# Prompt output rows and last states' keys: PE transposes replaced by VectorE 32x32 blocks and placing transfers to DRAM

## The chip, the cores and the metric

The kernel runs on one core of a Trainium2 chip. Time is device microseconds of that core for one launch; three runs of the kernel before gave a median of 2321.09 us (2320.81 to 2322.24).

## The reference

One decoder layer is computed for two groups of tokens that share the weights: a prompt of 256 tokens and 8 sequences of 8 sample tokens, 320 tokens in all, width 2048. Everything is float32.

```python
proj = jnp.einsum('btd,de->bte', x, w_in)          # q k v i f o | hq hf hi hg | two gates
h, C, n, m = _mlstm(q, k, v, ig, lf, C0, n0, m0)   # 4 heads, keys 256, values 512
h = _unheads((h - mu) * lax.rsqrt(var + LN_EPS)) * ml_norm_g
branch_a = h * jax.nn.sigmoid(ml_o)
o, S = _hgrn2(hq, jnp.log(f), 1.0 - f, hi, S0)     # 8 heads, keys 128, values 256
o = o * lax.rsqrt(jnp.mean(jnp.square(o), axis=-1, keepdims=True) + LN_EPS)
branch_b = _unheads(o) * hg_norm_g * jax.nn.silu(hg_g)
merged = jax.nn.sigmoid(gate_a) * (branch_a @ w_branch_a) + jax.nn.sigmoid(gate_b) * (branch_b @ w_branch_b)
x1 = _layernorm(alpha * x + merged @ w_out)
y = _layernorm(alpha * x1 + jnp.square(jax.nn.relu(x1 @ w_up)) @ w_down)
```

The outputs are `y` for both groups and the new states `C`, `n`, `m`, `S` for both groups. The prompt's last states are `C = (weighted K)^T V` and `S = (weighted K)^T I` over its 256 tokens.

## The kernel before

Activations lie with channels on the partitions and the 320 tokens along the row. A weight tile is 128 output columns; it comes in two units (halves) of 128x1024 values. For each unit SP loads `wr` (three buffers), ACT rounds it to a high part `wh`, DVE subtracts to get the low part `wl` (three pairs of buffers, called `bb` later, when there are more), and PE runs 24 matmuls of 320 columns: high by high, high by low, low by high, for each of 8 slices. A `wr` buffer is reloaded as soon as DVE has read it. This stream of 14,592 matmuls runs from start to end; everything else is fitted into it.

The fitting is done at build time by a small scheduler. Each piece of work (a head's output, a state update, an eviction) is a generator that yields instructions with an engine, an assumed cost and waits; the scheduler holds a model clock for each engine and issues a piece's next instruction between two groups of three matmuls once the model says that its inputs are there. So the order on each engine is fixed in the program, and real waits are semaphores. All transfers but a few go out on SP's queue in that order: weight reloads, state loads and stores, and the spills to DRAM named below.

Four places matter here, with the lines of the profile:

- **mLSTM output.** `m_num` (prompt rows) and `m_sample` (sample rows) of each of the 4 heads leave normalised rows in `hb`: three 128-token groups by 512 values. To turn them into channels by tokens, PE transposes 128x128 blocks into a PSUM bank (L1175, 12 for each head), ACT evicts them, multiplied by the norm weight `ml_norm_g`, and SP stores four tiles `hT` of 128x320.
- **HGRN2 output.** `h_out` of each of the 8 heads does the same from `on` (three groups by 256 values; L1610, 6 for each head), to tiles `oT`, with `hg_norm_g`.
- **Last states' keys.** `m_KW` weights the prompt's keys, PE turns them (L993, 4 for each mLSTM head), ACT and DVE split them into high and low parts `khl`, and `m_CP` stores them to `kD` with the values in `vD`. `h_sp` turns the HGRN2 keys (L1559, 2 for each head), ACT evicts them, and SP stores keys and values to `sD`. At the very end `m_C` (loads on POOL's queue) and `h_S` bring them back for the final state matmuls.
- **The gates.** Later `ev_o` (branch a) and `ev_hg` (branch b) evict the gate projections, take the stored tile that `fetch` has loaded and multiply the two.

Of the kernel before, what the change touches and what calls it, by code (L numbers as in the profile page):

```python
# [284 lines left out]


def by_row(ap, off, gap):

    return cap(ap, off, [[32, 4], [8, 2], [1, 8]] if gap else [[8, 4], [32, 2], [1, 8]])
# [16 lines left out]
class Program:  # L306
# [48 lines left out]
    def carve(self):  # L355
# [43 lines left out]
        self.pb = Pool([A(800)])  # L399
        self.ktk = Pool([A.three(2, 128)])  # L400
        self.it2 = [B.three(3, 256) for _ in range(2)]
# [221 lines left out]
    def start(self):  # L623
# [54 lines left out]
        self.gb_ev = [Ev() for _ in range(KT)]  # L678
        self.hT = [self.dr.tile([128, TOK], F32, name=f"hT{j}") for j in range(KT)]
        self.oT = [self.dr.tile([128, TOK], F32, name=f"oT{j}") for j in range(KT)]  # L680
        self.hT_ev = [Ev() for _ in range(KT)]
# [56 lines left out]
    def lb(self):  # L738

        nc = self.nc  # L740
        v = self.vec[:, V_LB:V_LB + 16].rearrange("p (r h) -> p r h", r=2)
        m = yield acq(self.sm)
        lb = self.lbv.rearrange("p (r h) -> p r h", r=2)
        e = m[:, 0:16].rearrange("p (r h) -> p r h", r=2)
        mx = m[:, 16:24]
        yield ("dve", 80, lambda: nc.vector.tensor_tensor(mx, v[:, 0], v[:, 1], ALU.max))
        yield ("dve", 80, lambda: nc.vector.tensor_tensor(e, v, mx.unsqueeze(1).to_broadcast([128, 2, 8]), ALU.subtract))
        yield ("act", 110, lambda: self.A(e, e, AF.Exp))
        yield ("dve", 80, lambda: nc.vector.tensor_tensor(mx, e[:, 0], e[:, 1], ALU.add))
# [3 lines left out]
        yield rel(self.sm, m)  # L753
        g, b = self.vec[:, V_G1:V_G1 + 16], self.vec[:, V_B1:V_B1 + 16]
# [80 lines left out]
    def m_start(self, h):  # L835
# [5 lines left out]
        m["v"] = [Ev() for _ in range(4)]  # L841
        for n in ("E", "S", "Vt", "Vs", "KW", "KH", "KS", "N", "CP", "QW", "bc_", "vst", "S0", "C", "ld"):
            m[n] = Ev()
# [132 lines left out]
    def m_KW(self, h):  # L976
# [12 lines left out]
        khl = yield acq(self.khl)  # L989
        b = yield acq(self.sbank)  # L990
        for i in range(2):
            for c in range(2):
                yield ("pe", PE_T, lambda: nc.tensor.transpose(b[:, 256 * i + 128 * c:256 * i + 128 * c + 128], kw[:, c, 128 * i:128 * i + 128], self.ident))  # L993
# [4 lines left out]
        yield ("dve", dve(512, True), lambda: v.tensor_tensor(kl, bv, kh.bitcast(F32), ALU.subtract))  # L998
        yield rel(self.sbank, b)
        yield post(m["KH"])  # L1000
# [55 lines left out]
    def m_num(self, h):  # L1056
# [15 lines left out]
        for i in range(2):  # L1072
# [25 lines left out]
    def m_C(self, h):  # L1098
        k = yield acq(self.kx)
        kt = yield ("pool", 1000, lambda: self.nc.gpsimd.dma_start(k, self.kD[h]))  # L1100
        w = yield acq(self.vx)
# [4 lines left out]
        for c in range(2):  # L1106
            if h:
                yield wait(self.ln[1]["fin"])
            b = yield acq(self.mbank)
            yield ("pe", 6 * pe_r(512), lambda: [self.mm(  # L1110
                b, k[:, x, s, 128 * c:128 * c + 128], w[:, y, s, :], start=n == 0, stop=n == 5)
                for n, (s, x, y) in enumerate((s, x, y) for s in range(2) for x, y in ((0, 0), (0, 1), (1, 0)))])
# [15 lines left out]
    def m_sample(self, h):  # L1128
# [41 lines left out]
        yield rel(self.sbank, nb)  # L1170
        yield rel(self.sm, dn)
        for j in range(4):
            b = yield acq(self.sbank)
            for i in range(3):
                yield ("pe", PE_T, lambda: nc.tensor.transpose(b[:, 128 * i:128 * i + 128], hb[:, i, 128 * j:128 * j + 128], self.ident))  # L1175
# [5 lines left out]
            yield rel(self.sbank, b)  # L1181
            yield ("sp", 620, lambda: self.dma(self.hT[jj], o))
            yield post(self.hT_ev[jj])
            yield wait(self.later())
            yield rel(self.tst, o)
        yield rel(self.hb, hb)
# [363 lines left out]
    def h_sp(self, h):  # L1550
# [5 lines left out]
        it, ks = m["it"], m["k"][:, 0:256]  # L1556
        b = yield acq(self.sbank)
        for i in range(2):
            yield ("pe", PE_T, lambda: nc.tensor.transpose(b[:, 128 * i:128 * i + 128], ks[:, 128 * i:128 * i + 128], self.ident))  # L1559
        kt = yield acq(self.ktk)  # L1560
        yield ("act", act(256, True), lambda: self.A(kt, b[:, 0:256].rearrange("p (a k) -> p a k", a=2)))
        yield rel(self.sbank, b)
# [3 lines left out]
        yield rel(self.ktk, kt)  # L1566
        yield post(m["SP"])

    def h_S(self, h):
        x = self.sx[h]  # L1570
        t = yield ("sp", 620, lambda: self.dma(x, self.sD[h]))
        e = Ev()
# [14 lines left out]
    def h_out(self, h):  # L1587
# [11 lines left out]
        for i in range(2):  # L1599
            yield from self.rms(b[:, 256 * i:256 * i + 256], on[:, i, :], 128)  # L1600
        yield rel(self.sbank, b)
        yield wait(m["S"])
        ob = m["ob2"]
        yield from self.rms(ob[:, 0:256], on[:, 2, :], 128)
        yield rel(self.sbank, ob)
        yield rel(self.at, at)
        for j in range(2):
            b = yield acq(self.sbank)
            for i in range(3):
                yield ("pe", PE_T, lambda: nc.tensor.transpose(b[:, 128 * i:128 * i + 128], on[:, i, 128 * j:128 * j + 128], self.ident))  # L1610
            jj = 2 * h + j
            o = yield acq(self.ho)
            g = self.vec[:, V_HGG + jj:V_HGG + jj + 1]
            yield ("act", act(NP_, True, 1), lambda: self.A(o[:, 0:NP_], b[:, 0:NP_], scale=g))
            yield ("act", act(64, True, 1), lambda: self.A(by_row(o, NP_, False), by_row(b, NP_, True), scale=g))
            yield rel(self.sbank, b)
            yield ("sp", 620, lambda: self.dma(self.oT[jj], o))
            yield post(self.oT_ev[jj])
            yield wait(self.later())
            yield rel(self.ho, o)  # L1620
        yield rel(self.on, on)
# [20 lines left out]
    def fetch(self, kind, j):  # L1642
# [4 lines left out]
        x = self.met[kind, j] = yield acq(self.ld)  # L1647
        e.t = yield ("sp", 620, lambda: self.dma(x, src[j]))

# [4 lines left out]
    def ev_o(self, j, c, b):  # L1654
# [32 lines left out]
    def ev_hg(self, j, c, b):  # L1687
# [7 lines left out]
        x = yield from self.fetched("hg", j)  # L1695
        yield ("dve", dve(TOK), lambda: v.tensor_tensor(g, g, x, ALU.mult))
        yield rel(self.ld, x)
# [256 lines left out]
    def run(self, pool):  # L1954
# [8 lines left out]
        self.vx, self.kx, self.main_end = Pool([]), Pool([]), Ev()  # L1963
        self.sD = [self.dr.tile([128, 768], F32, name=f"sD{j}") for j in range(HH)]
        self.kD = [self.dr.tile([128, 2, 2, 256], F32, name=f"kD{j}") for j in range(MH)]
        self.vD = [self.dr.tile([128, 2, 2, 512], F32, name=f"vD{j}") for j in range(MH)]
# [84 lines left out]
```

## Time and profile before

| What | Value |
| --- | --- |
| Median of 3 runs | 2321.09 us (2320.81 to 2322.24) |
| Profiled execution, its time | 2321.41 us |
| Its span | 2319.6 us |
| Granted TensorE clock, mean | 0.999 |
| Busy: PE, DVE, ACT, POOL | 2309.1, 1351.6, 1059.5, 11.9 us |
| DMA | 143275 packets, 424.92 MB, mean 183 GB/s |

All durations below come from the profiled execution, whose span is the time from its first to its last instruction. The stages in it: the mLSTM heads run beside the weight stream from about 75 to 440 us, the HGRN2 heads from about 440 to 860 us, then the gates and branch projections to about 1280 us, then the output projection and the feed-forward part to about 2292 us, and the last states with the final normalisation to the end.

### The profile page before, as it was taken

Reading aid. Unit: us, or ns where it says so; the run is one execution under the profiler, and the core shown is the slowest. Engines: PE = TensorE matmul, PEld = TensorE weight load, DVE = VectorE, ACT = ScalarE, POOL = GpSimd, SP = SyncE. Lnnn points to the kernel's source line nnn. Section 1 sums busy time; section 2 is a strip of 40 time slices with the busy share of each in tenths; the row PEclk is TensorE's granted clock in tenths of the full one; section 3 lists DMA queues with packets and bytes.
Section 4 is the critical chain, followed back from the end, with each engine's and each line's share of the span. In section 5 each row is a group of like instructions: output and inputs, shape, how many; then the busy total and the mean of one; then the engine's idle time right before and its main releaser. Section 6 shows DMA issues by size and latency. Waiting matters only on the chain.

```text
span 2319.6 us, 38982 instructions
## 1 busy us (share of the span) xinstructions
PE 2309.1 (100%) x15808; PEld 2267.0 (98%) x15808; DVE 1351.6 (58%) x2297; ACT 1059.5 (46%) x1703; POOL 11.9 (1%) x37
## 2 busy tenths in 40 slices
PE   9999999999999999999999999999999999999998
PEld 9999999999999999999999999999999999999997
DVE  6566567666666776555555767654444444444455
ACT  5444445555556565444433446533442343234333
POOL 0000000000000000000000000000000000000000
PEclk9999999999999999999999999999999999999999
DMA  7676777555555555555545654444444444444465
GB/s 282 206 254 223 269 280 230 193 187 181 183 181 188 182 189 172 174 177 169 176 169 176 213 167 152 150 146 154 146 155 146 154 147 154 146 153 147 153 219 182
DMA packets 143275, 424.92 MB, mean 183 GB/s; under 512 B 16372, under 2 KB 37748, under 8 KB 142072
## 3 DMA queue, kind: packets, MB, share of 16 engines
q1 hardware_dynamic: 141800, 415.96, 53.9%
q0 software_dynamic: 1152, 6.29, 0.8%
q8 instruction: 123, 2.02, 0.4%
q14 instruction: 56, 0.46, 0.1%
q10 hardware_dynamic: 144, 0.20, 0.0%
HBM read 371.48 MB, written 50.90 MB: 182 GB/s over the span
## 4 chain that ended last, share of the span: by engine, by line
PE 98%; ACT 1%; DVE 0%; DMA 0%; issue 0%; SPq 0%; ACTq 0%; DVEq 0%
PE bank L348 97%; ACT f3m L342 0%; DMA f<-first 0%; PE bank L1610 0%; PE bank L946 0%; PE bank L1175 0%; PE bank L1448 0%; DVE f3m L1938 0%; ACT f L342 0%; PE bank L1453 0%; PE bank L1019 0%; PE bank L1502 0%; PE bank L993 0%; PE bank L1559 0%; ACT oC L342 0%
## 5 line engine op out<-in xcount | busy, mean ns | idle before, releaser
L348 PE MATMUL bank<-xh,wh 128*128 128x320 f32 (+1 forms) x2432 | 782.4, 322 | 0.3 <-ACT wh L342 0.3
L488 DVE TENSOR_TENSOR wl<-wr,wh 128x1024 fp32r<-128x1024 f32 x426 | 522.0, 1225 | 399.6 <-ACT wh L342 395.9
L348 PE MATMUL bank<-xh,wl 128*128 128x320 f32 (+1 forms) x2432 | 752.2, 310 | 0.0
L348 PE MATMUL bank<-xl,wh 128*128 128x320 f32 (+1 forms) x2432 | 749.8, 309 | 0.0
L342 ACT ACTIVATE wh<-wr 128x1024 fp32r<-128x1024 f32 x426 | 451.0, 1059 | 498.1 <-PE bank L348 478.2
L348 PEld LDWEIGHTS bank<-xh,wh 128*128 128x128 f32 x2432 | 457.8, 188 | 19.2 <-issue 14.7
L348 PEld LDWEIGHTS bank<-xl,wh 128*128 128x128 f32 x2432 | 458.1, 189 | 2.9
L348 PEld LDWEIGHTS bank<-xh,wl 128*128 128x128 f32 x2432 | 458.0, 188 | 0.5 <-DVE wl L701 0.3
L488 DVE TENSOR_TENSOR bb<-wr,bb 128x1024 fp32r<-128x1024 f32 x176 | 215.7, 1226 | 229.2 <-ACT bb L342 229.1
L342 ACT ACTIVATE bb<-wr 128x1024 fp32r<-128x1024 f32 x176 | 186.4, 1059 | 313.3 <-PE bank L348 294.9
L348 PE MATMUL bank<-xh,bb 128*128 128x320 f32 (+1 forms) x1280 | 285.4, 309 | 0.0
L348 PE MATMUL bank<-rxb,bb 128*128 128x320 f32 x1208 | 276.3, 309 | 0.0
L348 PE MATMUL bank<-ra,wh 128*128 128x320 f32 x988 | 265.9, 308 | 0.0
L348 PE MATMUL bank<-ra,bb 128*128 128x320 f32 x1096 | 264.2, 308 | 0.7 <-DVE ra L1640 0.7
L348 PEld LDWEIGHTS bank<-xh,bb 128*128 128x128 f32 x1280 | 215.0, 188 | 0.0
L348 PEld LDWEIGHTS bank<-rxb,bb 128*128 128x128 f32 x1208 | 204.3, 188 | 0.2
L348 PE MATMUL bank<-xl,bb 128*128 128x320 f32 (+1 forms) x640 | 197.7, 309 | 0.0
L348 PEld LDWEIGHTS bank<-ra,bb 128*128 128x128 f32 x1096 | 187.1, 188 | 1.2 <-DVE ra L1640 0.9
L348 PEld LDWEIGHTS bank<-ra,wh 128*128 128x128 f32 x988 | 176.3, 188 | 0.0
L348 PE MATMUL bank<-rxb,wh 128*128 128x320 f32 x548 | 169.0, 308 | 0.0
L348 PE MATMUL bank<-rxb,wl 128*128 128x320 f32 x548 | 169.0, 308 | 0.0
L348 PEld LDWEIGHTS bank<-xl,bb 128*128 128x128 f32 x640 | 120.4, 188 | 0.3 <-DVE xl L1863 0.3
(263 smaller groups left out, 2233.9 us busy)
## 6 DMA issues: line engine op xcount, KB each, us to landing
wr<-wt SPq DMA_DIRECT2D x602, 512.0 KB, 3.4
rx<-C SPq DMA_DIRECT2D x34, 256.0 KB, 5.6
Cs<-rx SPq DMA_DIRECT2D x34, 256.0 KB, 4.4
f<-C SPq DMA_DIRECT2D x30, 256.0 KB, 5.3
Cs<-f SPq DMA_DIRECT2D x30, 256.0 KB, 4.8
f<-first SPq DMA_DIRECT2D x6, 704.0 KB, 10.8
vD<-ra SPq DMA_DIRECT2D x4, 1024.0 KB, 6.8
f<-S SPq DMA_DIRECT2D x8, 512.0 KB, 6.6
```

Source lines behind the costliest of these rows:

```text
L342: return self.nc.scalar.activation(out, in_, func, **kw)
L348: self.nc.tensor.matmul(*a, **kw)
L488: self.V().tensor_tensor(lo, raw, hi.bitcast(F32), ALU.subtract)
```

## The change

The prompt's rows no longer go through PE. DVE transposes each 32x32 block inside a tile in place (`v.transpose`); a 128x128 tile is then right inside its 16 blocks but the blocks are in the wrong places. `place` puts them right on the way to DRAM: four transfers, one for each band of 32 partitions, write every 32-value piece of a partition (128 bytes) to its place in a "home" of 128x128 tiles. The sample rows keep their PE transposes and go to small tensors `hL` and `oL`, one transfer for each head in place of the four or two that carried the tiles. A consumer now loads a tile with two transfers, 256 pieces of 512 bytes from `hH` or `oH` and 128 pieces of 256 bytes from `hL` or `oL`. The keys of the last states take the same way: `kD` and `sD` become homes, the HGRN2 values get their own tensor `iD`. The norm weights move from ACT's evictions to the multiplications in `ev_o` and `ev_hg`; `ml_norm_g` is negated once at the start, since `ev_o` had a factor of -1 there.

The diff, without the plain renames and allocations:

```diff
+def cap2(ap, off, dims):
+    return bass.AP(ap.tensor, ap.offset + off, [list(x) for x in dims])
...
+        home = lambda name, heads: [self.dr.tile([2, D // heads, 128], F32, name=f"{name}{j}") for j in range(heads)]
+        tail = lambda name, heads: [self.dr.tile([D // heads, 64], F32, name=f"{name}{j}") for j in range(heads)]
...
+    def place(self, to, x):
+
+        for a in range(4):
+            yield ("sp", 620, lambda: self.dma(to(a), x[32 * a:32 * a + 32]))
+
+    def rows_to(self, home):
+
+        return lambda a: cap2(home, 32 * a, [[128, 32], [32 * 128, home.shape[1] // 16], [1, 32]])
...
         khl = yield acq(self.khl)
-        b = yield acq(self.sbank)
-        for i in range(2):
-            for c in range(2):
-                yield ("pe", PE_T, lambda: nc.tensor.transpose(b[:, 256 * i + 128 * c:256 * i + 128 * c + 128], kw[:, c, 128 * i:128 * i + 128], self.ident))
         m["khl"] = khl
         kh, kl = khl[:, 0], khl[:, 1]
-        bv = b.rearrange("p (a k) -> p a k", a=2)
-        yield ("act", act(512, True), lambda: self.A(kh, bv))
-        yield ("dve", dve(512, True), lambda: v.tensor_tensor(kl, bv, kh.bitcast(F32), ALU.subtract))
-        yield rel(self.sbank, b)
+        yield ("dve", dve(512), lambda: v.transpose(kw[:, :, 0:256], kw[:, :, 0:256]))
+        yield ("act", act(512), lambda: self.A(kh.rearrange("p s k -> p (s k)").rearrange("p (c t) -> p c t", c=2), kw[:, :, 0:256]))
+        yield ("dve", dve(512), lambda: v.tensor_tensor(kl, kw[:, :, 0:256], kh.bitcast(F32), ALU.subtract))
...
             yield rel(self.sbank, b)
+            yield ("dve", dve(512), lambda: v.transpose(hb[:, i, :], hb[:, i, :]))
         yield rel(self.sbank, db)
         yield post(m["N"])
+        yield from self.place(self.rows_to(self.hH[h]), hb[:, 0:2, :].rearrange("p i v -> p (i v)").rearrange("p (b c) -> p b c", c=32))
+        m["hb_"].t = self.s.lands[-1]
...
-        yield ("sp", 620, lambda: self.dma(self.kD[h], m["khl"].bitcast(F32)))
+        x = m["khl"].bitcast(F32).rearrange("p x s k -> p (x s k)").rearrange("p (B k) -> p B k", k=32)
+        yield from self.place(lambda a: cap2(self.kD[h], 32 * a, [[128, 32], [32 * 128, 32], [1, 32]]), x)
...
-        kt = yield ("pool", 1000, lambda: self.nc.gpsimd.dma_start(k, self.kD[h]))
+        kt = yield ("pool", 1000, lambda: self.nc.gpsimd.dma_start(
+            k.rearrange("p x s k -> p (x s k)").rearrange("p (y k) -> p y k", k=128), self.kD[h].rearrange("y p k -> p y k")))
...
+        b = yield acq(self.sbank)
         for j in range(4):
-            b = yield acq(self.sbank)
-            for i in range(3):
-                yield ("pe", PE_T, lambda: nc.tensor.transpose(b[:, 128 * i:128 * i + 128], hb[:, i, 128 * j:128 * j + 128], self.ident))
-            jj = 4 * h + j
-            o = yield acq(self.tst)
-            g = self.vec[:, V_MLG + jj:V_MLG + jj + 1]
-            yield ("act", act(NP_, True, 1), lambda: self.A(o[:, 0:NP_], b[:, 0:NP_], scale=g))
-            yield ("act", act(64, True, 1), lambda: self.A(by_row(o, NP_, False), by_row(b, NP_, True), scale=g))
...
-            yield ("sp", 620, lambda: self.dma(self.hT[jj], o))
+            yield ("pe", PE_T, lambda: nc.tensor.transpose(b[:, 128 * j:128 * j + 128], hb[:, 2, 128 * j:128 * j + 128], self.ident))
+        o = yield acq(self.tst)
+        for j in range(4):
+            yield ("act", act(64, True), lambda: self.A(by_row(o, 64 * j, False), by_row(b, 128 * j, True)))
+        yield rel(self.sbank, b)
+        yield ("sp", 620, lambda: self.dma(
+            self.hL[h].rearrange("(j p) t -> p j t", p=128), o[:, 0:256].rearrange("p (j t) -> p j t", t=64)))
...
-        for i in range(2):
-            yield ("pe", PE_T, lambda: nc.tensor.transpose(b[:, 128 * i:128 * i + 128], ks[:, 128 * i:128 * i + 128], self.ident))
-        kt = yield acq(self.ktk)
-        yield ("act", act(256, True), lambda: self.A(kt, b[:, 0:256].rearrange("p (a k) -> p a k", a=2)))
...
-        yield ("sp", 620, lambda: self.dma(self.sD[h][:, 0:256], kt))
-        yield ("sp", 620, lambda: self.dma(self.sD[h][:, 256:768], it[:, 0:2, :]))
+        yield ("dve", dve(256), lambda: v.transpose(ks, ks))
+        yield from self.place(lambda a: cap2(self.sD[h], 32 * a, [[128, 32], [32 * 128, 8], [1, 32]]),
+                              ks.rearrange("p (b k) -> p b k", k=32))
+        yield ("sp", 620, lambda: self.dma(self.iD[h], it[:, 0:2, :]))
...
+        for i in range(2):
+            yield ("dve", dve(256), lambda: v.transpose(on[:, i, :], on[:, i, :]))
+        yield from self.place(self.rows_to(self.oH[h]), on[:, 0:2, :].rearrange("p i v -> p (i v)").rearrange("p (b c) -> p b c", c=32))
...
+        if isinstance(src[j], tuple):
+            y, z = src[j]
+            yield ("sp", 620, lambda: self.dma(x[:, 0:NP_].rearrange("p (i t) -> p i t", i=2), y.rearrange("i p t -> p i t")))
+            e.t = yield ("sp", 620, lambda: self.dma(x[:, NP_:TOK], z))
...
-        yield ("dve", dve(TOK), lambda: v.scalar_tensor_tensor(g, g, -1.0, x, ALU.mult, ALU.mult))
+        yield ("dve", dve(TOK, ptr=1), lambda: v.scalar_tensor_tensor(g, g, self.vec[:, V_MLG + j:V_MLG + j + 1], x, ALU.mult, ALU.mult))
```

The instruction order shows what this does to the engines. On PE, in the first mLSTM head's output, the order before has this stretch; L1175 are output transposes and L993 key transposes, both removed or thinned, L946 are transposes of the values, which stay, and L348 is the weight stream:

```order
L1175 MATMUL bank_88<-cst,f_77 128x128
L993 MATMUL bank_84<-cst,f_76 128x128
L348 MATMUL bank_83<-xh,wh 128x320
L348 MATMUL bank_83<-xl,wh 128x320
L348 MATMUL bank_83<-xh,wl 128x320
L946 MATMUL bank_87<-cst,f_75 128x128
L1175 MATMUL bank_88<-cst,f_77 128x128
L348 MATMUL bank_83<-xh,wh 128x320
```

In the changed program the same head's output has only the sample rows' transposes (now L1191), and the weight stream (now L352) runs six matmuls between two of them:

```order
L1191 MATMUL bank_88<-cst,f_77 128x128
L352 MATMUL bank_83<-xh,wh 128x320
L352 MATMUL bank_83<-xl,wh 128x320
L352 MATMUL bank_83<-xh,wl 128x320
L352 MATMUL bank_83<-xh,wh 128x320
L352 MATMUL bank_83<-xl,wh 128x320
L352 MATMUL bank_83<-xh,wl 128x320
L1191 MATMUL bank_88<-cst,f_77 128x128
```

Over the whole program PE has 96 transposes fewer and no other instruction more or less.

On SP's queue, at the first mLSTM head's key store, the order before is:

```order
L351 DMA gaD_148<-f_76 128x320
L351 DMA kD_100<-ra 128x1024
L351 DMA vD_104<-ra 128x2048
L351 DMA wr<-wt 128x1024 x2
L351 DMA Cs<-f_77 128x512 x2
```

and in the changed program, at the same place:

```order
L355 DMA gaD_156<-f_76 128x320
L355 DMA kD_108<-ra 32x32x32 x4
L355 DMA vD_112<-ra 128x2048
L355 DMA wr<-wt 128x1024 x2
L355 DMA Cs<-f_77 128x512 x2
```

Four transfers of 1024 pieces each stand where one of 128 pieces stood, ahead of the values (`vD`) and of the next two weight reloads (`wr`). A little later on SP's queue, where the first head's prompt rows are ready, the order before has state traffic (`C` loads, `Cs` stores) and reloads:

```order
L351 DMA wr<-wt 128x1024
L351 DMA f_77<-C 128x512 x2
L351 DMA wr<-wt 128x1024 x6
L351 DMA Cs<-f_77 128x512 x2
L351 DMA wr<-wt 128x1024
```

The changed program has the four transfers to the home `hH` there, between the fifth and the sixth of these reloads:

```order
L355 DMA wr<-wt 128x1024
L355 DMA f_77<-C 128x512 x2
L355 DMA wr<-wt 128x1024 x5
L355 DMA hH_187<-f_77 32x32x32 x4
L355 DMA wr<-wt 128x1024
L355 DMA Cs<-f_77 128x512 x2
L355 DMA wr<-wt 128x1024
```

The stores of the tiles `hT`, which came later one by one, are gone. The weight reloads keep their order among themselves.

More of the change, by code (lines that the diff above doesn't have):

```diff
@@ L678, in start @@
         self.gb_ev = [Ev() for _ in range(KT)]
-        self.hT = [self.dr.tile([128, TOK], F32, name=f"hT{j}") for j in range(KT)]
-        self.oT = [self.dr.tile([128, TOK], F32, name=f"oT{j}") for j in range(KT)]
+        home = lambda name, heads: [self.dr.tile([2, D // heads, 128], F32, name=f"{name}{j}") for j in range(heads)]
+        tail = lambda name, heads: [self.dr.tile([D // heads, 64], F32, name=f"{name}{j}") for j in range(heads)]
+        self.hH, self.oH, self.hL, self.oL = home("hH", MH), home("oH", HH), tail("hL", MH), tail("oL", HH)
+        rows = lambda homes, tails: [(x[:, j:j + 128, :], y[j:j + 128, :]) for x, y in zip(homes, tails) for j in range(0, y.shape[0], 128)]
+        self.hT, self.oT = rows(self.hH, self.hL), rows(self.oH, self.oL)
         self.hT_ev = [Ev() for _ in range(KT)]
@@ L841, in m_start @@
         m["v"] = [Ev() for _ in range(4)]
-        for n in ("E", "S", "Vt", "Vs", "KW", "KH", "KS", "N", "CP", "QW", "bc_", "vst", "S0", "C", "ld"):
+        for n in ("E", "S", "Vt", "Vs", "KW", "KH", "KS", "N", "CP", "QW", "bc_", "vst", "S0", "C", "ld", "hb_"):
             m[n] = Ev()
@@ L1110, in m_C @@
             yield ("pe", 6 * pe_r(512), lambda: [self.mm(
[L1111 removed]
+                b, k.rearrange("p x s k -> p (x s k)")[:, 512 * x + 256 * c + 128 * s:512 * x + 256 * c + 128 * s + 128], w[:, y, s, :], start=n == 0, stop=n == 5)
                 for n, (s, x, y) in enumerate((s, x, y) for s in range(2) for x, y in ((0, 0), (0, 1), (1, 0)))])
@@ L1171, in m_sample @@
         yield rel(self.sm, dn)
+        b = yield acq(self.sbank)
         for j in range(4):
[L1173 to L1185 removed]
+            yield ("pe", PE_T, lambda: nc.tensor.transpose(b[:, 128 * j:128 * j + 128], hb[:, 2, 128 * j:128 * j + 128], self.ident))
[5 more added lines that the diff above has]
+            self.hL[h].rearrange("(j p) t -> p j t", p=128), o[:, 0:256].rearrange("p (j t) -> p j t", t=64)))
+        for j in range(4):
+            yield post(self.hT_ev[4 * h + j])
+        yield wait(self.later())
+        yield rel(self.tst, o)
+        yield wait(m["hb_"])
         yield rel(self.hb, hb)
@@ L1601, in h_out @@
         yield rel(self.sbank, b)
+        for i in range(2):
+            yield ("dve", dve(256), lambda: v.transpose(on[:, i, :], on[:, i, :]))
+        yield from self.place(self.rows_to(self.oH[h]), on[:, 0:2, :].rearrange("p i v -> p (i v)").rearrange("p (b c) -> p b c", c=32))
+        done = self.later()
         yield wait(m["S"])
@@ L1606, in h_out @@
         yield rel(self.at, at)
+        b = yield acq(self.sbank)
         for j in range(2):
[L1608 to L1620, printed above, removed]
+            yield ("pe", PE_T, lambda: nc.tensor.transpose(b[:, 128 * j:128 * j + 128], on[:, 2, 128 * j:128 * j + 128], self.ident))
+        o = yield acq(self.ho)
+        for j in range(2):
+            yield ("act", act(64, True), lambda: self.A(by_row(o, 64 * j, False), by_row(b, 128 * j, True)))
+        yield rel(self.sbank, b)
+        yield ("sp", 620, lambda: self.dma(
+            self.oL[h].rearrange("(j p) t -> p j t", p=128), o[:, 0:128].rearrange("p (j t) -> p j t", t=64)))
+        for j in range(2):
+            yield post(self.oT_ev[2 * h + j])
+        yield wait(self.later())
+        yield rel(self.ho, o)
+        yield wait(done)
         yield rel(self.on, on)
@@ L1963, in run @@
         self.vx, self.kx, self.main_end = Pool([]), Pool([]), Ev()
-        self.sD = [self.dr.tile([128, 768], F32, name=f"sD{j}") for j in range(HH)]
-        self.kD = [self.dr.tile([128, 2, 2, 256], F32, name=f"kD{j}") for j in range(MH)]
+        self.sD = [self.dr.tile([2, 128, 128], F32, name=f"sD{j}") for j in range(HH)]
+        self.iD = [self.dr.tile([128, 2, 256], F32, name=f"iD{j}") for j in range(HH)]
+        self.kD = [self.dr.tile([8, 128, 128], F32, name=f"kD{j}") for j in range(MH)]
         self.vD = [self.dr.tile([128, 2, 2, 512], F32, name=f"vD{j}") for j in range(MH)]
```

14 lines of the change are left out of this document (7 added, 7 removed).

## Prediction

> **What bounds the kernel now.** I read the page first. It gives the span, the busy times, the chain that ended last and the transfer queue that carries nearly everything.
>
> ```profile
> span 2319.6 us, 38982 instructions
> PE 2309.1 (100%) x15808; PEld 2267.0 (98%) x15808; DVE 1351.6 (58%) x2297; ACT 1059.5 (46%) x1703; POOL 11.9 (1%) x37
> q1 hardware_dynamic: 141800, 415.96, 53.9%
> PE 98%; ACT 1%; DVE 0%; DMA 0%; issue 0%; SPq 0%; ACTq 0%; DVEq 0%
> ```
>
> PE is busy for all but 10.5 us of the span and makes 98% of the chain. The list of PE's waits says the same from the other side; these three rows are all of it:
>
> ```profile
> PE bank L348 <- POOL ones L631: 1.0, 1, 1.0
> PE bank L348 <- DVE ra L1640: 0.7, 1, 0.7
> PE bank L348 <- ACT wh L342: 0.3, 1, 0.3
> ```
>
> So PE is the bound in every stage, and an instruction taken from it shortens the kernel by the time that it holds the array, as long as the weights keep coming. What must not happen is that the weight stream runs dry. How far ahead it is, the timelines of DVE, SP and ACT show in the mLSTM stage (start, duration, instruction). DVE has read a `wr` buffer at 299.15 + 1.23 = 300.38, SP reloads that buffer at 300.40, and two other buffers are rounded before it, the second at 305.55; its turn is 309.64.
>
> ```profile
> 299.15 1.23 DVE L488 TENSOR_TENSOR wl<-wr,wh 128x1024 fp32r<-128x1024 f32 x1 [0.21 <-ACT wh L342]
> ...
> 300.40 0.34 SPq L351 DMA_DIRECT2D wr<-wt  x1
> ...
> 305.55 1.05 ACT L342 ACTIVATE wh<-wr 128x1024 fp32r<-128x1024 f32 x1
> ...
> 309.64 1.06 ACT L342 ACTIVATE wh<-wr 128x1024 fp32r<-128x1024 f32 x1
> ```
>
> The list of transfers gives sizes and the median time from issue to landing, and its summary for all of L351 the shortest:
>
> ```profile
> wr<-wt SPq DMA_DIRECT2D x602, 512.0 KB, 3.4
> vD<-ra SPq DMA_DIRECT2D x4, 1024.0 KB, 6.8
> gbD<-f SPq DMA_DIRECT2D x16, 160.0 KB, 2.5
> DMA to landing us min/median/max: 1.8/3.4/13.4
> ```
>
> A reload may land 309.64 - 300.40 - 3.4 = 5.8 us later than it does before ACT waits for it. ACT's turn comes when PE frees a pair of three, so PE then still has two units of 24 matmuls at 0.145 us (next fence), 7.0 us, less 1.06 for ACT, 1.23 for DVE and a tenth between: 4.6 us. **Cover: 5.8 + 4.6 = 10.4 us** of delay to a weight reload before PE stands still.
>
> **The 96 transposes that go.** The groups by line:
>
> ```profile
> L1610 PE MATMUL bank<-cst,f 128*128 128x128 f32 x48 | 13.1, 272 | 0.0
> L1175 PE MATMUL bank<-cst,f 128*128 128x128 f32 x48 | 13.0, 271 | 0.0
> L993 PE MATMUL bank<-cst,f 128*128 128x128 f32 x16 | 4.3, 272 | 0.0
> L1559 PE MATMUL bank<-cst,f 128*128 128x128 f32 x12 | 3.3, 272 | 0.0
> ```
>
> Of L1175 and L1610 the sample rows' 16 each stay, 32 each go; L993 goes with 16, L1559 with 16 (12 here and 4 in a second group, for the heads whose set lies in `f3h`). That is 96. The 272 ns are a duration in a pipeline, in which neighbours overlap. The time that one holds PE is read from starts, in PE's timeline:
>
> ```profile
> 303.85 0.31 PE L348 MATMUL bank<-xl,wh 128*128 128x320 f32 x1
> ...
> 305.30 0.31 PE L348 MATMUL bank<-xh,wl 128*128 128x320 f32 x1
> ...
> 306.29 0.31 PE L348 MATMUL bank<-xh,wl 128*128 128x320 f32 x1
> 306.44 0.27 PE L946 MATMUL bank<-cst,f 128*128 128x128 f32 x1
> 306.55 0.27 PE L1175 MATMUL bank<-cst,f 128*128 128x128 f32 x1
> 306.58 0.39 PE L348 MATMUL bank<-xh,wh 128*128 128x320 f32 x1
> 306.81 0.31 PE L348 MATMUL bank<-xl,wh 128*128 128x320 f32 x1
> ```
>
> Ten plain steps take 305.30 - 303.85 = 1.45, 0.145 each. From 306.29 to 306.81 there are two such steps and two transposes: 0.52 - 0.29 = 0.23, 0.115 for each. L946 is a transpose of the same form. Sum: 96 x 0.115 = **11.0 us less**, all on the path.
>
> The Trainium skill, "TensorE: Matmul & The Clock Gate", Part 4, gives about 275 ns for a transpose among other work; by that figure the sum would be 96 x 0.275 = 26.4 us. The trace has it as the duration (272 ns), but the starts show 0.115 us, and I go by the starts.
>
> **DVE's 36 new transposes**, 12 of 512 and 24 of 256 columns. None is in the trace; the nearest rows are plain passes of the same widths:
>
> ```profile
> L1041 DVE TENSOR_SCALAR f<-f,misc 128x512 f32<-128x512 f32 x12 | 6.5, 546 | 0.4
> L998 DVE TENSOR_TENSOR ra<-bank,ra 128x512 fp32r<-128x512 f32 x4 | 2.8, 692 | 3.0 <-ACT ra L342 3.0
> L900 DVE TENSOR_TENSOR f<-f,cst 128x256 f32<-128x256 f32 x4 | 1.6, 408 | 0.0
> ```
>
> At 0.55 to 0.69 for 512 and half of 0.55 to 0.41 for 256 they are 13 to 18 us. The two head stages have room:
>
> ```profile
> 75.00:440.00 365.00, 365.00 (x2508) 341.02 (x2508) 233.02 (x459) 168.63 (x283) 2.47 (x7) 1.00 0.71 242
> 480.00:860.00 380.00, 380.00 (x2692) 371.49 (x2691) 261.65 (x633) 228.51 (x498) 1.84 (x5) 1.00 0.57 185
> ```
>
> (window, its length, then busy PE, PEld, DVE, ACT, POOL, the clock, DMA share, GB/s). DVE is free for 132 and 118 us there, and one transpose ahead of a weight's subtraction delays it by 0.7 us at most, against 4.6 of cover. I take 0; without cover it would be the 13 to 18 us. A gain is excluded: DVE isn't the bound. ACT loses evictions and gains one small negation: 0 for the same reason. The weights in `ev_o` and `ev_hg` ride on passes that are there already.
>
> **The placing transfers.** This is the open price. Each mLSTM head now has two bursts (`kD`, `hH`) of four transfers with 1024 rows of 128 bytes, each HGRN2 head one of 4 x 512 (`oH`) and one of 4 x 256 (`sD`). Bytes hardly change. By bytes: queue q1 moves 415.96 MB in 0.539 x 2319.6 = 1250 us, 333 GB/s, so a burst of 512 KB takes 1.6 us, as the single transfer did. By rows: the same 1250 us on 16 engines over 141800 packets are 0.141 us a packet; if a 128-byte row cost that, 64 rows an engine would be 9.0 us a transfer, 36 us a burst. In between, `gbD` has 128 rows and lands in 2.5 us; less the shortest landing of 1.8 and its 160 KB at 333 GB/s (0.49), 0.21 us remain for 128 rows, 1.6 ns each. Then 1024 rows are 1.7 + 0.4 = 2.1 us, a burst 8.4, an `oH` burst 4.2, an `sD` burst 2.1. I take this one, since it is the row with the least other work in it.
>
> Behind the burst on SP's queue stand the weight reloads, and PE waits for those after 10.4 us. A burst of 8.4 is covered. After `kD` comes `vD`, 1024 KB or 3.1 us more, 11.5 in all, less some 2 us that SP takes to issue the five: about at the cover. I take 1 us over the four heads, ends 0 and what the rivals say. The first transfer of `hH` also waits for DVE's transpose, with reloads queued behind; SP waits like that today for up to 4.9 us at one time, without a stall on PE:
>
> ```profile
> SPq L351 <- DVE misc L1048: 89.0, 24, 4.9
> ```
>
> `oH` and `sD` cost 0 by the same cover.
>
> **The loads back.** Two transfers for a tile in place of one, 384 rows for 128: 256 x 1.6 ns = 0.4 us, asked for while the weight stream of their own tile still runs. 0. The key loads at the end go out on POOL with 1024 rows in place of 128; POOL's and PE's timelines:
>
> ```profile
> 2280.69 0.54 POOL L1100 DMA_DIRECT2D wh<-kD  x1 [29.41 <-PE bank L348]
> ...
> 2297.25 1.52 PE L348 MATMUL bank<-bb,wh 128*128 128x512 f32 x6
> ```
>
> This is the first load of the last pair, and the second follows it; they have 16 us. Even at eight times 0.54 for each issue, 8.6 for both, 7 us are left to land. 0; with both at the row price of 9 us it would be 1 to 2.
>
> **Sum.** 2321.41 (the profiled execution; 1.8 of it lies outside the span) - 11.0 + 1 = 2311.4. That execution was 0.3 above the median, so I say **2311.0**. About 0.2% (4.6 us) is what a measurement of this kernel can tell from no change.
>
> **Rivals.**
>
> *Placing starves the weights (slower).* Place: the eight bursts of the mLSTM stage, where DMA share is already 0.71. With p us for a transfer of 1024 rows, PE loses 8 x (4p - 10.4). It decides from p = 2.9 on, where this eats the 11.0. At p = 4: 8 x 5.6 = 45 us, time 2355. For it: no row this short is in the trace in number, and 2.9 is not far from 2.1. Against: the `gbD` row. Chance 0.22; the lower third of it ends below 2345.
>
> *A row of 128 bytes costs as much as a mean packet.* p = 9: 8 x 25.6 = 205 and 8 x (18 - 10.4) = 61 for `oH`, so 2576. Against: 36 us is six times what the bytes and the `gbD` row allow. Chance 0.04. The Trainium skill, "VectorE: DVE Perf Modes", The three transpose paths, warns that a plain DMA that transposes by strides is 19 times slower; by that a burst would be 19 x 1.6 = 30 us, near this rival. Here the innermost run is 32 values, not one, and no run so far shows it.
>
> *The bursts just overrun the cover*, p from 2.4 to 2.9: the gain is mostly eaten, 2317 to 2321. Chance 0.06.
>
> *A transpose holds PE for its whole duration:* 96 x 0.272 = 26 us less, 2295. Against: the starts above. Chance 0.02.
>
> *The change doesn't do what it says:* the freed slots aren't filled, because the weights are no sooner ready. Against: PE's waits total 2.0 us, and the stream has 4.6 us in hand. It would give 2321; it is within the third rival's chance.
>
> **How the numbers follow.** My forecast (bursts covered, 2309 to 2316) has 0.66; the rivals 0.22, 0.04, 0.06, 0.02. The range runs from 2309.0 (2321.1 - 96 x 0.12 = 2309.6 with no stall, and half a microsecond for the two-digit starts) to 2345.0 (p = 3.7), which holds 0.66 + 0.06 + a third of 0.22 = 0.79. Faster by over 0.2% is 0.66 + 0.02 = 0.68, within it 0.06, slower 0.22 + 0.04 = 0.26.
>
> **What would show it.** Right: PE's busy time about 11 us lower, PE's waits still a few us, transfers of `hH` and `kD` landing within about 4 us of issue, ACT's rounding never waiting long for `wr`. Wrong: ACT or PE waiting on `wr` between 75 and 440 us in steps of several us after each burst, landings of 6 us and more for a 128 KB transfer, SP stuck in issuing, or DVE transposes above 0.7 us.

## The result, and the profile after

The changed kernel takes 2311.3 us (median, 2310.47 to 2311.95) beside 2321.09 before: a ratio of 0.9957, 95% interval 0.9947 to 0.9967, which is 9.8 us less, between 7.7 and 12.3. The profiled execution took 2310.56 us. The page of the changed kernel has span, busy times, transfer queue and chain:

```profile
span 2308.7 us, 38882 instructions
PE 2299.2 (100%) x15712; PEld 2258.4 (98%) x15712; DVE 1365.3 (59%) x2333; ACT 1040.1 (45%) x1664; POOL 13.3 (1%) x37
q1 hardware_dynamic: 209512, 415.97, 55.7%
PE 99%; ACT 1%; DVE 0%; issue 0%; ACTq 0%; POOL 0%; DVEq 0%; POOLq 0%
```

PE is busy 9.9 us less with 96 instructions less, and is still the whole chain. The queue has 67712 packets more for the same bytes. PE's waits are these two rows, 1.7 us; ACT's waits for a raw weight unit are the next fence (us in total, times, longest). Before they were 7.1 and 4.5 us in total. The longest now, 3.6 us, did not reach PE: the weight stream did not run dry.

```profile
PE bank L352 <- POOL ones L634: 1.0, 1, 1.0
PE bank L352 <- DVE ra L1657: 0.7, 1, 0.7
```

```profile
ACT bb L346 <- DMA wr<-wt: 6.3, 5, 2.1
ACT wh L346 <- DMA wr<-wt: 4.3, 3, 3.6
```

The groups by line show what DVE does in PE's place, 0.70 to 0.71 us for 512 columns and 0.43 to 0.44 for 256; two smaller groups of these, 8 more transposes in all, are left out:

```profile
L1086 DVE STREAM_TRANSPOSE f<-f 128x512 f32<-128x512 f32 x8 | 5.7, 708 | 0.2
L1000 DVE STREAM_TRANSPOSE f<-f 128x512 f32<-128x512 f32 x4 | 2.8, 701 | 0.0
L1616 DVE STREAM_TRANSPOSE f<-f 128x256 f32<-128x256 f32 x16 | 6.7, 430 | 0.2 <-ACT f L346 0.2
```

The list of transfers (KB each, median us from issue to landing), and for `kD` the view of its tile (duration of the issue in ns, min/median/max):

```profile
wr<-wt SPq DMA_DIRECT2D x602, 512.0 KB, 3.4
vD<-ra SPq DMA_DIRECT2D x4, 1024.0 KB, 5.6
kD<-ra SPq DMA_DIRECT2D x16, 128.0 KB, 3.9
hH<-f SPq DMA_DIRECT2D x16, 128.0 KB, 3.8
oH<-f SPq DMA_DIRECT2D x32, 64.0 KB, 3.3
```

```profile
L355 SPq DMA_DIRECT2D kD<-ra x16: 340/598/4544, 87.7 to 339.4; - x16
L1107 POOL DMA_DIRECT2D wh<-kD x2: 898/963/1028, 2238.7 to 2270.4; - x2
```

A transfer of 1024 rows lands in 3.8 to 3.9 us in the median (single ones took up to 7.1 for `kD` and 6.3 for `hH`), and a weight reload still in 3.4. SP takes 0.6 us to issue a `kD` transfer, once 4.5; POOL takes 0.96 us for a key load in place of 0.54. The windows of the two head stages, and the last of the `gaD` stores, which is issued at the end of the mLSTM stage (first and last start are the two figures in us; it stood at 449.7 before):

```profile
75.00:440.00 365.00, 365.00 (x2498) 341.22 (x2497) 243.38 (x479) 163.66 (x272) 2.47 (x7) 1.00 0.78 244
480.00:860.00 380.00, 380.00 (x2677) 372.18 (x2676) 272.29 (x664) 220.84 (x480) 1.83 (x5) 1.00 0.60 187
```

```profile
L355 SPq DMA_DIRECT2D gaD<-f x16: 326/327/1032, 80.5 to 444.2; - x16
```

DMA share rose from 0.71 to 0.78 and from 0.57 to 0.60. Of the time gained, 5.5 us were there by the end of the mLSTM stage.

### The profile page after: what moved, and what is told of

Same layout as the page of the kernel before. It is cut to its first block, busy times and chain, and to the rows that moved or that the text cites. A ratio compares the mean times of both kernels' runs of the same rounds, so it can differ in the third digit from the quotient of the medians.

```text
span 2308.7 us, 38882 instructions
## 1 busy us (share of the span) xinstructions
PE 2299.2 (100%) x15712; PEld 2258.4 (98%) x15712; DVE 1365.3 (59%) x2333; ACT 1040.1 (45%) x1664; POOL 13.3 (1%) x37
## 3 DMA queue, kind: packets, MB, share of 16 engines
q1 hardware_dynamic: 209512, 415.97, 55.7%
## 4 chain that ended last, share of the span: by engine, by line
PE 99%; ACT 1%; DVE 0%; issue 0%; ACTq 0%; POOL 0%; DVEq 0%; POOLq 0%
PE bank L352 98%; ACT f3m L346 0%; PE bank L954 0%; PE bank L1465 0%; DVE f3m L1960 0%; ACT f L346 0%; PE bank L1470 0%; PE bank L1519 0%; PE bank L1022 0%; PE bank L1626 0%; PE bank L1191 0%; ACT oC L346 0%; ACT oS L346 0%; ACT bb L346 0%; ACT xh L346 0%
## 5 line engine op out<-in xcount | busy, mean ns | idle before, releaser
L352 PE MATMUL bank<-xh,wh 128*128 128x320 f32 (+1 forms) x2432 | 781.3, 322 | 0.0
L352 PE MATMUL bank<-xh,wl 128*128 128x320 f32 (+1 forms) x2432 | 752.2, 310 | 0.0
L352 PE MATMUL bank<-xl,wh 128*128 128x320 f32 (+1 forms) x2432 | 750.0, 309 | 0.0
L352 PEld LDWEIGHTS bank<-xh,wh 128*128 128x128 f32 x2432 | 458.1, 189 | 18.0 <-issue 15.5
L352 PEld LDWEIGHTS bank<-xl,wh 128*128 128x128 f32 x2432 | 458.4, 189 | 3.3
L352 PEld LDWEIGHTS bank<-xh,wl 128*128 128x128 f32 x2432 | 458.0, 188 | 0.2 <-DVE wl L491 0.2
L352 PE MATMUL bank<-xh,bb 128*128 128x320 f32 (+1 forms) x1280 | 285.4, 309 | 0.0
L352 PE MATMUL bank<-rxb,bb 128*128 128x320 f32 x1208 | 276.3, 309 | 0.0
L352 PE MATMUL bank<-ra,wh 128*128 128x320 f32 x988 | 265.9, 309 | 0.0
L352 PE MATMUL bank<-ra,bb 128*128 128x320 f32 x1096 | 264.3, 309 | 0.7 <-DVE ra L1657 0.7
L352 PEld LDWEIGHTS bank<-xh,bb 128*128 128x128 f32 x1280 | 215.0, 188 | 0.0
L352 PEld LDWEIGHTS bank<-rxb,bb 128*128 128x128 f32 x1208 | 204.2, 188 | 0.2
L352 PE MATMUL bank<-xl,bb 128*128 128x320 f32 (+1 forms) x640 | 197.7, 309 | 0.0
L352 PEld LDWEIGHTS bank<-ra,bb 128*128 128x128 f32 x1096 | 187.1, 188 | 1.2 <-DVE ra L1657 0.9
L352 PEld LDWEIGHTS bank<-ra,wh 128*128 128x128 f32 x988 | 176.3, 188 | 0.0
L352 PE MATMUL bank<-rxb,wh 128*128 128x320 f32 x548 | 169.0, 308 | 0.0
L352 PE MATMUL bank<-rxb,wl 128*128 128x320 f32 x548 | 169.0, 308 | 0.0
L352 PEld LDWEIGHTS bank<-xl,bb 128*128 128x128 f32 x640 | 120.4, 188 | 0.2 <-DVE xl L1885 0.2
```

The source lines that it names most:

```text
L352: self.nc.tensor.matmul(*a, **kw)
```

## Experiments

The times are medians, the ratios are to the kernel before, run on the same chip. The kernel before had medians of 2320.99 to 2321.09 us on these chips. "Over the changed kernel" is the difference from 2311.3.

**The price of a transpose, first try.** 96 unread transposes go back where the old ones stood, into banks of the shared pool:

```diff
+    def idle_t(self, count, x):
+        b = yield acq(self.sbank)
+        for n in range(count):
+            yield ("pe", PE_T, lambda: self.nc.tensor.transpose(b[:, 128 * n:128 * n + 128], x(n), self.ident))
+        yield rel(self.sbank, b)
...
+        yield from self.idle_t(4, lambda n: kw[:, n // 2, 128 * (n % 2):128 * (n % 2) + 128])
```

> The changed kernel with the 96 PE transposes put back at their old places, into a PSUM bank that nothing reads; the placing transfers, VectorE's transposes and everything else stay as changed. Theory (the gain is the time that the transposes hold PE, 0.115 us each): 96 x 0.115 = 11.0 us come back, 2311.3 + 11.0 = about 2322, the time of before. Rival (the gain comes from ACT's lighter load, fewer PSUM banks held and fewer weight-side delays): the time stays near 2311, at most 2314.

Measured: 2331.01 us, ratio 1.0042 (1.0028 to 1.0056), 19.7 over the changed kernel. Neither figure. PE's waits in this run:

```profile
PE bank L1023 <- DVE f L982: 3.4, 1, 3.4
PE bank L954 <- DVE ra L958: 0.8, 1, 0.8
```

Both lie in one hole, from 256.25 us on, in which PE starts no weight matmul for 12.5 us: transposes of several pieces stand together there. Most likely the extra claims on banks had moved the fixed order, but that was not tested. So this run priced a reordering along with the transposes. It is inconclusive, and the next one repeats it at a quiet place.

**The price of a transpose, second try.** The same 96, of the identity, beside the weight stream of the gates, where banks are free:

```diff
+        if kind == "o" and h >= 4:
+            s.spawn(self.idle_t(8), 6)
```

> The changed kernel with 96 idle PE transposes (of the identity, eight to one PSUM bank, read by nobody) put beside the weight stream of the gates, where PE's PSUM banks are free and no other order moves but the numbers of banks. Theory (a transpose among the stream holds PE for 0.115 us, so 96 are 11.0 us): 2322.3, about the time of before. Rival 1 (a transpose holds PE for its 272 ns): 2311.3 + 26.1 = 2337.4. Rival 2 (transposes fill gaps that are there anyway and the gain came from elsewhere): 2311 to 2313. PE's busy time should rise from 2299.2 by 11 under the theory.

Measured: 2323.12 us, ratio 1.0009 (1.0000 to 1.0017), 11.8 over the changed kernel, 0.123 us for each. PE's busy time rose by 11.7 us, from 2299.2 to 2310.9. This is another stage than that of the old transposes, but the price is close to the 0.115 us that the starts gave there. PE's timeline shows one:

```profile
904.99 0.31 PE L352 MATMUL bank<-xh,wl 128*128 128x320 f32 x1
905.14 0.27 PE L1142 MATMUL bank<-cst 128*128 128x128 f32 x1
905.17 0.39 PE L352 MATMUL bank<-xh,wh 128*128 128x320 f32 x1
905.40 0.31 PE L352 MATMUL bank<-xl,wh 128*128 128x320 f32 x1
```

Two plain steps and a transpose take 905.40 - 904.99 = 0.41 us, so the transpose takes 0.41 - 0.29 = 0.12, though its own row says 0.27. The theory of the occupied slot holds. That the array is held for the whole duration (2337.4) is refuted, and so is that the slots were free anyway.

**The keys alone.** The kernel before with only the last states' keys changed (`m_KW`, `m_CP`, `h_sp` and the loads of `m_C` and `h_S`), 32 transposes fewer:

```diff
-                yield ("pe", PE_T, lambda: nc.tensor.transpose(b[:, 256 * i + 128 * c:256 * i + 128 * c + 128], kw[:, c, 128 * i:128 * i + 128], self.ident))
+        yield ("dve", dve(512), lambda: v.transpose(kw[:, :, 0:256], kw[:, :, 0:256]))
...
-        yield ("sp", 620, lambda: self.dma(self.kD[h], m["khl"].bitcast(F32)))
+        yield from self.place(lambda a: cap2(self.kD[h], 32 * a, [[128, 32], [32 * 128, 32], [1, 32]]), x)
```

> The kernel before with only the last states' keys changed (kD, sD, iD); output rows still go through PE. 32 transposes fewer. Theory: 32 x 0.115 = 3.7 us less, 2317.4 (2316.5 to 2318.5). Rival (the placing of the keys, which has the values' 1024 KB behind it in the queue, eats part of its gain): 2319 or more.

Measured: 2319.27 us, ratio 0.9993 (0.9984 to 1.0002): 1.7 us less (between 3.7 less and 0.5 more) where 32 x 0.123 = 3.9 went from PE. The theory's range is missed and the rival's figure met. Waits of PE's weight loads name what came late, the old states of the sample sequences, `C` (0.5 us in one wait before):

```profile
PEld bank L352 <- DMA rx<-C: 4.1, 10, 0.9
PEld bank L352 <- DMA f<-C: 1.1, 4, 0.3
```

**The rows alone.** The changed kernel with the old way for the keys, 64 transposes fewer than before; the edit is the one above, undone.

> The kernel before with only the prompt output rows changed (hH, oH, hL, oL and the norm weights at the gates); keys still go through PE. 64 transposes fewer. Theory: 64 x 0.115 = 7.4 us less, 2313.7 (2313 to 2315), and with the keys alone it adds up to the whole. Rival (one part carries all of the gain, the other none): 2311 or 2321.

Measured: 2314.52 us, ratio 0.9971 (0.9961 to 0.9982): 6.5 us less where 64 x 0.123 = 7.9 went. Most of the gain is here. The two parts add up to 8.2, the whole gave 9.8; the intervals are too wide to call that a difference.

**Placing twice, three and six times.** Each placing transfer is followed by copies of itself to scratch tensors:

```diff
             yield ("sp", 620, lambda: self.dma(to(a), x[32 * a:32 * a + 32]))
+            for n in range(2):
...
+                yield ("sp", 620, lambda: self.dma(bass.AP(copy.tensor, copy.offset + o.offset % 128, [list(d) for d in o.ap]), x[32 * a:32 * a + 32]))
```

> The changed kernel with every placing transfer issued twice, the second time to scratch DRAM. Tripled it cost 17.7 us, sixfold 73.6, all in the mLSTM stage and for late state loads. Theory (there is a cover that one burst does not use up): 2311 to 2316, PE's waits still under 4 us; from 17.7 and 73.6 a straight line of 18.6 us per extra copy through them meets zero at 2.05 times, so most likely 2312. Rival (each copy costs from the first on, and the change itself already pays for one): 2311.3 + 17.7/2 = 2320 with PE waiting for state loads, and then the placing of the change would cost some 9 us too, which the measured gain leaves no room for unless the transposes were worth 20 us.

> The changed kernel with every placing transfer issued three times, twice more into scratch tensors that nothing reads: three times the rows and bytes, PE's program the same. In the changed kernel's trace a burst of four transfers with 1024 rows takes about 3.4 to 4.4 us when nothing stands between them. Theory (a cover of about 10 us before PE stands still): three times 4 are 12 us, just over it, in the eight mLSTM bursts: 0 to 5 us each, so 2311 to 2330, most likely about 2316. Rival (the cover is much smaller and the placing already costs PE time): tripling it adds as much as the bursts' own added time, 8 x 8 = 64 us and more, 2375. Rival (the placing has a bandwidth of its own and never reaches the weights): 2311.

> As before with six times the placing transfers. Theory: a burst of 24 us less 10.4 of cover is 13 us in each of eight bursts, and an oH burst of about 12 us less 10.4 is 2 us in each of eight: 8 x 13 + 8 x 2 = 120 us, about 2430. Rival (no cover): 8 x 20 + 8 x 10 = 240 us and more, 2550. Rival (never reaches the weights): 2311.

| Placed | Time, us | Ratio to before | Over the changed kernel |
| --- | --- | --- | --- |
| once | 2311.3 | 0.9957 (0.9947 to 0.9967) | 0 |
| twice | 2320.46 | 0.9998 (0.9989 to 1.0007) | 9.2 |
| three times | 2329.03 | 1.0033 (1.0021 to 1.0046) | 17.7 |
| six times | 2384.85 | 1.0277 (1.0262 to 1.0292) | 73.6 |

For each: the window of the mLSTM stage, the last `gaD` store, and the waits of PE's weight loads. Twice:

```profile
75.00:440.00 365.00, 360.95 (x2423) 332.80 (x2422) 235.66 (x464) 156.77 (x262) 2.47 (x7) 1.00 0.83 250
```

```profile
L355 SPq DMA_DIRECT2D gaD<-f x16: 320/327/1599, 80.3 to 454.8; - x16
```

```profile
PEld bank L352 <- DMA f<-C: 4.8, 6, 1.7
PEld bank L352 <- DMA rx<-C: 2.3, 1, 2.3
PEld bank L352 <- DVE wl L491: 1.2, 2, 1.0
PEld bank L352 <- ACT wh L346: 1.1, 1, 1.1
```

Three times (the profiled execution, 2333.24 us, was the slowest of the six):

```profile
75.00:440.00 365.00, 353.28 (x2342) 321.70 (x2341) 229.06 (x455) 151.54 (x253) 0.61 (x3) 0.99 0.89 256
```

```profile
L355 SPq DMA_DIRECT2D gaD<-f x16: 326/521/3005, 80.5 to 466.7; - x16
```

```profile
PEld bank L352 <- DMA f<-C: 9.2, 5, 4.6
PEld bank L352 <- DMA rx<-C: 7.9, 3, 4.2
PEld bank L352 <- DVE wl L491: 1.2, 2, 1.0
```

Six times:

```profile
75.00:440.00 365.00, 326.81 (x2060) 289.25 (x2059) 192.09 (x389) 131.15 (x221) 0.00 (x0) 0.95 0.99 247
```

```profile
L355 SPq DMA_DIRECT2D gaD<-f x16: 326/479/2434, 80.4 to 516.5; - x16
```

```profile
PEld bank L352 <- DMA rx<-C: 16.4, 5, 11.0
PEld bank L352 <- DMA f<-C: 13.8, 6, 4.6
PEld bank L1196 <- DVE f L1044: 8.3, 3, 7.4
```

The rows of the transfer queue, for twice, three and six times:

```profile
q1 hardware_dynamic: 268392, 423.31, 57.5%
q1 hardware_dynamic: 327272, 430.66, 58.8%
q1 hardware_dynamic: 503912, 452.70, 64.6%
```

Three readings. First, the place: placed twice, three and six times, the last `gaD` store is 10.6, 22.5 and 72.3 us later than in the changed kernel, and the profiled executions are 10.1, 22.7 and 73.1 us longer, so nearly all of the loss lies in the mLSTM stage. `oH` and `sD` cost next to nothing, even sixfold. Second, what is late: state loads. Twice, they make 7.1 of the 9.4 us in these rows, three times 17.1 of 18.3; a late weight unit (`wl`, `wh`) makes the rest. Six times, other waits join them. Third, the size: by q1's share of the span, its packets took 1286 us in the changed kernel (55.7% of 2308.7) and 1333, 1371 and 1539 us here. The copies are as many rows as 56, 112 and 280 transfers of 1024, so one takes 0.85, 0.76 and 0.90 us of the 16 engines: about 0.8 us, and a burst of four about 3.3. The DMA share of the window alone would give less (0.05 of 365 us for 32 transfers, 0.57 each), because less of the weight stream fits into the same 365 us, 2423 of PE's instructions in place of 2498.

My expectations were poor. The tripled kernel came out at the upper end of its theory's 2311 to 2330, not near the likely 2316, and the sixfold one 45 us under its theory's 2430, far from both rivals. For the doubled kernel mine was wrong. The straight line through three and six times has no basis, since the cost per copy is not constant: 9.2, 8.5, then 18.6 for each of the last three. The rival's 2320 was hit, but its second half, that the first placing then also pays some 9 us, doesn't fit: 96 x 0.123 - 9.8 leaves 2.0 for it. So the changed kernel stands close to the knee, the amount of placing from which PE begins to stand.

**Whose time is it, SP's or the DMA engines'?** The copies of the tripled kernel are issued by POOL on its own queue:

```diff
-                yield ("sp", 620, lambda: self.dma(bass.AP(copy.tensor, ...
+                yield ("pool", 1000, lambda: self.nc.gpsimd.dma_start(bass.AP(copy.tensor, ...
```

> As the run with tripled placing transfers, the same 2 scratch copies of each, but the copies are issued by POOL on its own queue; the transfers that count stay on SP. Tripled on SP it cost 17.7 us over the changed kernel, as PE waited for state loads. Theory A (the state loads come late because SP issues one transfer after another and the copies stand in front of them): the cost goes, 2311 to 2315, PE waits under 4 us. Theory B (the rows of 128 bytes take the DMA engines' own time, whoever issues them): 2325 to 2333, PE waits for state loads as before. In between, say 2317 to 2323, both have a share.

Measured: 2338.64 us, ratio 1.0076 (1.0062 to 1.0089), 27.3 over the changed kernel, 9.6 more than with the copies on SP. Waits of PE's weight loads, and transfers:

```profile
PEld bank L352 <- DMA rx<-C: 12.7, 4, 4.9
PEld bank L352 <- DMA f<-C: 10.9, 5, 4.2
```

```profile
copy<-ra POOLq DMA_DIRECT2D x32, 128.0 KB, 7.4
copy<-f POOLq DMA_DIRECT2D x32, 128.0 KB, 7.1
hH<-f SPq DMA_DIRECT2D x16, 128.0 KB, 7.1
```

Theory A's figure is missed: the state loads are late without copies on SP's queue, too. Theory B gave 2325 to 2333 and fell short. On POOL's queue a copy lands in 7.1 to 7.4 us, and the `hH` transfers beside them in 7.1 in place of 3.8. So the queue changes the transfer itself, and the run doesn't price the engines alone. Nor does it free SP of a share in the runs before. In the doubled kernel's chain, issues on SP stand right before a late state load (start, duration, what):

```profile
210.87 0.82 SPq L355
211.73 0.49 SPq L355
212.27 6.01 DMA f<-C
218.32 13.76 PE bank L352 x85
```

The second of these issues is a copy's. How much of the loss is SP's issuing and how much the engines' time stays open, and so does whether the stores that free the loads' buffers are late as well.

**The placing that counts on POOL's queue,** for the mLSTM heads (`kD`, `hH`):

```diff
+    def place_pool(self, to, x):
+        for a in range(4):
+            yield ("pool", 1000, lambda: self.nc.gpsimd.dma_start(to(a), x[32 * a:32 * a + 32]))
```

> The changed kernel with the placing transfers of the mLSTM heads (kD, hH: 32 transfers) issued by POOL in place of SP. The 96 transposes measured 11.8 us when put back at a quiet place, the change gained 9.8, so some 2 us are lost to the rest. Theory A (they are lost on SP's queue): 2309.3 to 2310.3. Theory B (on the DMA engines, or not at all): 2311.3, within 0.8. Rival: POOL's transfers are slower to start and the buffers hb and khl come free later, so that state work or values wait: 2313 or more, with new PE waits.

Measured: 2313.13 us (2311.69 to 2314.63), ratio 0.9966 (0.9953 to 0.9978), 1.8 over the changed kernel. Not faster: nothing is won by taking them off SP's queue. The rival's figure is met, just, though the interval overlaps that of the changed kernel. PE's weight loads wait 1.7 us for `f<-C` in place of 0.8; whether buffers come free later, as the rival says, is not shown.

**The sample rows too.** The last 32 transposes go the same way: DVE turns the sample rows, and placing transfers with rows of 64 bytes write them to `hL` and `oL`. The tokens then stand in another order, which the multiplications in `ev_o` and `ev_hg` undo, three passes for one:

```diff
-            yield ("pe", PE_T, lambda: nc.tensor.transpose(b[:, 128 * j:128 * j + 128], hb[:, 2, 128 * j:128 * j + 128], self.ident))
+        yield ("dve", dve(512), lambda: v.transpose(hb[:, 2, :], hb[:, 2, :]))
+        yield from self.place(self.tail_to(self.hL[h]), cap(hb[:, 2, :], 0, [[32, 16], [1, 16]]))
```

> The changed kernel with the sample rows treated the same way: VectorE transposes them too, and four placing transfers with rows of 64 bytes put them into hL and oL, with the tokens in another order that the gates' multiplication undoes (three smaller VectorE passes in place of one). 32 more PE transposes go, and their evictions. Theory: 32 x 0.115 = 3.7 us less than the changed kernel, 2307.6. Rival (SP's queue and the small rows have used up the cover in the mLSTM stage): 2311 or more.

Measured: 2307.90 us (2307.72 to 2308.23), ratio 0.9943 (0.9931 to 0.9956): 3.4 less than the changed kernel, as 32 x 0.115 = 3.7 asks. This is the fastest version.

**The two together,** the kernel just shown with its mLSTM prompt rows and keys placed by POOL:

> The kernel that also turns the sample rows on DVE (2307.9 us), with the placing transfers of the mLSTM heads' prompt rows and keys issued by POOL. Theory A: 2305.9 to 2306.9, and this would be the fastest. Theory B: 2307.9, within 0.8. Rival (buffers come free later): 2310 or more.

Measured: 2310.66 us, ratio 0.9957 (0.9944 to 0.9971). A loss again, 2.8 us beside the kernel just shown; the rival's figure is met, its reason is not shown.

## Why the prediction was right

- **"96 x 0.115 = 11.0 us less, all on the path."** Measured at a quiet place 0.123 each, 11.8 in all; the span fell by 10.9. The right step was to read starts, not durations. The Trainium skill, "TensorE: Matmul & The Clock Gate", Part 4, gives about 275 ns for a bf16 transpose in one kernel's context; here, in float32, that is the duration (272 ns), while the time taken from PE's other work is 0.12 us.
- **"+1 us over the four heads."** 11.8 less the 9.8 gained leaves 2.0; with the interval of the gain it is anything from 0 to 4. The two profiled executions show less, 11.8 - 10.9 = 0.9. In the mLSTM stage, where the prediction put its 1 us, 48 transposes went, worth 5.9 us, and 5.5 were gained by the last `gaD` store. The keys alone lost 2.2 of their 3.9, give or take 2, so which transfer costs what in the whole change stays open.
- **"1024 rows are 2.1 us, a burst 8.4."** Mis-sized: about 0.8 and 3.3 us, twice the end by bytes (0.4 and 1.6). The 0.21 us drawn from the landing of `gbD` are not the price of its 128 rows; at 0.8 us for 1024 these would be 0.1. The error lay on the safe side. The rival with a mean packet's cost (9 us a transfer) is refuted; the 36 us of its burst were 4.3 times my 8.4, not six. The 19 times that the Trainium skill, "VectorE: DVE Perf Modes", The three transpose paths, sets on a transpose by plain DMA are against the DMA's own transpose, where the innermost destination stride is large; with an innermost run of 32 values they do not appear.
- **"Cover: 10.4 us."** This step failed, though the time didn't suffer. It was read for the weight reloads, but the state loads run short first. A doubled burst is about 6.6 us and a tripled one 9.9, both under 10.4, and yet PE lost 9.2 / 8 = 1.15 and 2.2 us a burst, mostly waiting for state loads. No single cover fits: 6.6 - 1.15 = 5.5, 9.9 - 2.2 = 7.7, and 19.8 - 9.2 = 10.6 for six times. The burst of 8.4 us that I had taken lies between twice and three times, so it would have cost an estimated 9 to 18 us, the whole gain or more. The time came out right because two errors offset each other, which is luck: the burst was taken as 2.5 times too long and the cover as too large. The bursts were covered, as forecast, but not by the margin that I had worked out.
- **"The bursts just overrun the cover, p from 2.4 to 2.9."** By my own sum the loss begins at p = 2.6 (4 x 2.6 = 10.4) and reaches 2317 only at 2.8. With p at 0.8 this rival, like the one in which placing starves the weights, did not come about.
- **"DVE's 36 transposes, 13 to 18 us, 0 on the path."** They are 12 x 0.71 + 24 x 0.43 = 18.8 us, a little above the top end. More than 0.7 us for one was named as a sign of being wrong; 0.70 to 0.71 is just there, and it had no effect, since DVE is busy 243 of 365 us in the mLSTM stage and no wait of PE names a transpose. Landings of over 6 us were another such sign; a few came, without a wait of PE over 0.3 us for them.
- **The loads back at the end, 0.** POOL needs 0.9 to 1.0 us for each of the four issues, so about 1.8 of the 16 us for the last pair; no wait of PE names these loads.

## What to carry over

Price what is taken from a saturated PE by the starts of its neighbours, and check that price where nothing else moves; an instruction put back into a tight static order can price the order instead. When a transfer is added to a busy stage, work out the cover of every kind of load that PE waits for there, not only of the biggest stream: here the smaller loads that stand in a fixed order ran short first. Doubling the added transfer is a cheap way to see how far off the knee is.

## What the runs showed of the hardware

- A DMA write in 128-byte pieces costs about twice what its bytes would: about 0.8 us of the 16 engines for 1024 pieces (128 KB), beside 0.4 at the queue's mean rate.
- On SP's queue these pieces count as one packet each. With the mLSTM placing on POOL's queue, q1 falls by 33280 packets and q0 rises by only 1536, yet the same transfers land in 6.4 us (`kD`) and 5.2 (`hH`) in place of 3.9 and 3.8:

```profile
q1 hardware_dynamic: 176232, 411.77, 53.8%
q0 software_dynamic: 6272, 10.49, 2.0%
```

- DVE's 32x32 transpose of a float32 tile takes 0.70 to 0.71 us for 512 columns and 0.43 to 0.44 for 256, dearer than one plain pass of 512 columns (0.55), close to another (0.69).
